# A hybrid decoder trunk in float32: the table load for Exp and Ln is queued behind all Silus of the mixers

## The chip, the cores and the metric

The kernel runs on one core of one Trainium2 chip. The metric is the device time of one execution in microseconds (us); the time before is the median of three runs. Durations come from one profiled execution of the same program. In the profile PE is TensorE's matmuls, PEld its weight loads, DVE is VectorE, ACT is ScalarE, POOL is GpSimd. L384 is line 384 of the kernel.

## The reference

The input is one sequence of 256 tokens of width 1024 in float32. Two layers follow each other; each is

```python
x = x + 0.5 * swiglu(rms_norm(x, ffn1_norm), w_gate, w_up, w_down)      # inner width 2816
P = rms_norm(x, mix_norm) @ w_in                                        # 3608 columns, cut among four mixers
y = concat[gla(P_a), fox(P_b), ssd(P_c), short_conv(P_d)] @ w_out
x = x + y
x = x + 0.5 * swiglu(rms_norm(x, ffn2_norm), w_gate, w_up, w_down)
```

The mixers need two families of functions. Silu is wanted four times in the state-space mixer and the gated linear attention: on the convolved columns of x, B and C (`silu(conv(xbc) + b)`), on the gate z, and on the gate g of the linear attention. Exp and Ln are wanted in all four mixers: softplus (as max(w, 0) + ln(1 + exp(-|w|))), the decays, the softmax of the forgetting attention, and the inverse root of every headwise RMS norm (exp(-0.5 ln(.))).

## The kernel before, in words

Everything lies with features on the partitions and the 256 tokens in the free dimension. Each weight block of 128x1024 float32 is loaded by SyncE's queue, rounded by ScalarE to a high part `wh` (the CAST at L120) and reduced by VectorE to the rest `wl` (L122); a product is then three matmuls of rounded parts: high by high, high by low, low by high (`mm3`, L138; `wide`, L155 and L158, for the feed-forward parts). These two operations for each block run through the whole kernel.

A layer is `ffn`, `mixing`, `ffn`. `mixing` walks through 15 projections in the order PROJ (c_x, c_B, c_C, small, c_z, a_g, b_q, ...). After each projection is traced, `advance()` lets each of five Python generators (`narrow`, `ssd`, `fox`, `gla`, `shortconv`) trace its next piece, up to its next `yield`. So the mixers' small work stands among the projections' matmuls. That is only the order in which the program is traced. The order on each engine is made by a planner that simulates the program (`schedule_with_timeline_sim=True`, L1016) and moves instructions within what the data and extra order edges allow. An extra edge is made by `tc.issue_after(ins)`: what is traced in its block is queued behind `ins` on the engine of `ins`. `tc.keep_in_program_order(ins)` queues `ins` behind the one instruction of its engine that was traced last. Each engine then works its queue in order.

ScalarE looks up a function in the table set that is active. A load of a set is an instruction of its own (ACT_TABLE_LOAD). Three kinds of them stand in the program. The kernel asks for two itself: the set of Silu at the start (L82), and in each layer `natural_log_exp_and_others` by `load_exp_ln` (L379 and L380). The others are put in after the planner, ahead of an instruction whose function the active set does not serve; the profile gives them the line of that instruction (L322, L484 for Silu, L384 for Exp and Ln).

The part of a mixer that matters here, in the order of tracing:

- `ssd` (L473): `conv(i)` (L477) does two blocks of 128 columns each: a scaling on ScalarE (L480), three multiply-adds on VectorE (L482), Silu on ScalarE (L484). `conv(0)`, `conv(1)`, `conv(2)` are traced while the projections c_C, small and c_z stand in line; then follow the Silu of z (L497), that of g (L500), and `load_exp_ln()` (L501), which is thereby pinned behind the Silu of g alone. It then sets `ready["exp"]`.
- `narrow` (L449) waits for `ready["exp"]` and traces the softplus of the narrow columns (L457: Abs at L389, Exp, Ln, then VectorE at L392), the coefficient (L459), the product and scan that give `cs` (L461, L462), `Ra` (L466), and four scalings that give `La` (L468).
- Every Exp and Ln goes through `expln` (L382), which queues it behind the load.
- `ssd` then multiplies `La` with `Ra` on TensorE (L537); `fox` makes its scores, their row maximum `mx` (L631), the exponentials `pr` (L634, shown under L384) and their transposes on TensorE (L643).

Of the kernel before, what the change touches and what calls it, by code (L numbers as in the profile page):

```python
# [11 lines left out]
AF = mybir.ActivationFunctionType  # L12
# [50 lines left out]
def tile_kernel(tc, xT, W, WS, gains, params, consts, out):  # L63
    nc = tc.nc
    with ExitStack() as ctx:
# [8 lines left out]
        V, S, TE = nc.vector, nc.scalar, nc.tensor  # L74
# [299 lines left out]
            return xn  # L374


        loaded = [None]

        def load_exp_ln():  # L379
            loaded[0] = tc.keep_in_program_order(S.preload_act_table_set("natural_log_exp_and_others")).ins  # L380

        def expln(*args, **kw):  # L382
            with tc.issue_after(loaded[0]):
# [11 lines left out]
        def mixing(l, xs):  # L395
# [9 lines left out]
            def P(name, n=1, i=0):  # L405
                o = PCOL[name] + i
                return par[:, l, o:o + n]

            def wait(name):
                while name not in ready:  # L410
                    yield

            def evict(name, dst=None, **kw):
                if dst is None:
                    dst = t2(name, **kw)
                V.tensor_tensor(dst, ready[name], bc2(rbc), op=ALU.mult)
                return dst
# [55 lines left out]
            def ssd():  # L473
# [3 lines left out]
                def conv(i):  # L477
                    for c in (2 * i, 2 * i + 1):
                        a = xbc[:, c, :]
                        S.activation(a, U[:, c, 0:T], AF.Copy, scale=P("cw", 1, c))  # L480
                        for k in range(1, 4):
                            V.scalar_tensor_tensor(a, U[:, c, k:k + T], P("cw", 1, 6 * k + c), a,  # L482
                                                   op0=ALU.mult, op1=ALU.add)
                        S.activation(a, a, AF.Silu, bias=P("cb", 1, c))  # L484

                for i, name in enumerate(("c_x", "c_B")):
                    yield from wait(name)
                    evict(name, U[:, 2 * i:2 * i + 2, 3:])
                conv(0)
                yield from wait("c_C")  # L490
                evict("c_C", U[:, 4:6, 3:])
                conv(1)
                yield
                conv(2)
                yield from wait("c_z")
                sz = evict("c_z")
                S.activation(sz, sz, AF.Silu)  # L497
                yield from wait("a_g")
                sg = sh["sg"] = evict("a_g")
                S.activation(sg, sg, AF.Silu)  # L500
                load_exp_ln()  # L501
                ready["exp"] = True
                yield from wait("cs")
# [266 lines left out]
            def shortconv():  # L770
# [21 lines left out]
                y[3] = hilo(yd)  # L792

            mixers = [narrow(), ssd(), fox(), gla(), shortconv()]

            def advance():
# [224 lines left out]
```

## Time and profile before

| | |
|---|---|
| median of three runs | 1038.33 us (1036.86, 1038.33, 1040.24) |
| the profiled execution | 1035.23 us |
| its span, first to last instruction | 1033.4 us |
| mean granted TensorE clock over the span | 0.995 |
| busy share PE, DVE, ACT | 98%, 74%, 59% |
| first mixing stage, about | 200 to 332 us of the span |
| second mixing stage, about | 712 to 840 us of the span |

A timeline row reads: start, length, engine, line, operation, out<-in, shapes, count, and in brackets the idle time of the engine ahead of it and what ended that. A row with a count above one joins neighbours, so its length is that of the whole.

### The profile page before, as it was taken

Reading aid. Unit: us, or ns where it says so; the run is one execution under the profiler, and the core shown is the slowest. Engines: PE = TensorE matmul, PEld = TensorE weight load, DVE = VectorE, ACT = ScalarE, POOL = GpSimd, SP = SyncE. Lnnn points to the kernel's source line nnn. Section 1 sums busy time; section 2 is a strip of 40 time slices with the busy share of each in tenths; the row PEclk is TensorE's granted clock in tenths of the full one; section 3 lists DMA queues with packets and bytes.
Section 4 is the critical chain, followed back from the end, with each engine's and each line's share of the span. In section 5 each row is a group of like instructions: output and inputs, shape, how many; then the busy total and the mean of one; then the engine's idle time right before and its main releaser. Section 6 shows DMA issues by size and latency. Waiting matters only on the chain.

```text
span 1033.4 us, 16590 instructions
## 1 busy us (share of the span) xinstructions
PE 1014.7 (98%) x6424; PEld 911.8 (88%) x6424; DVE 763.9 (74%) x1192; ACT 612.8 (59%) x928; POOL 1.8 (0%) x6
## 2 busy tenths in 40 slices
PE   7999999999999999999999999999999999999998
PEld 5888888998989888888888888889989998888887
DVE  7987856695877888775688877567868779877652
ACT  6655644469768665554365555344798676555430
POOL 0000000000000000000000000000000000000000
PEclk9999999999999999999999999999999999999999
DMA  8756555372435466554656555564624337665550
GB/s 294 265 196 186 188 197 186 104 258 88 144 102 164 151 222 196 186 186 145 219 187 200 184 185 186 180 204 131 217 93 136 120 122 242 194 188 191 185 180 24
DMA packets 62462, 181.52 MB, mean 176 GB/s; under 512 B 5808, under 2 KB 6960, under 8 KB 62384
## 3 DMA queue, kind: packets, MB, share of 16 engines
q1 hardware_dynamic: 62240, 180.44, 52.9%
q8 instruction: 50, 0.82, 0.3%
q14 instruction: 28, 0.23, 0.1%
q10 hardware_dynamic: 144, 0.02, 0.0%
HBM read 179.40 MB, written 1.05 MB: 175 GB/s over the span
## 4 chain that ended last, share of the span: by engine, by line
PE 91%; ACT 6%; DVE 2%; issue 1%; DMA 0%; ACTq 0%; DVEq 0%
PE acc L155 29%; PE ps L155 18%; PE acc L158 15%; PE ps L138 9%; PE ps L158 9%; PE acc L138 7%; ACT wh L120 2%; ACT L384 1%; DVE wl L122 1%; PE acc L654 1%; DMA x<-xT 0%; PE acc L718 0%; PE acc L537 0%; PE acc L643 0%; PE acc L626 0%
## 5 line engine op out<-in xcount | busy, mean ns | idle before, releaser
L120 ACT CAST wh<-st 128x1024 fp32r<-128x1024 f32 (+1 forms) x339 | 352.2, 1047 | 323.8 <-PE acc L155 135.7
L122 DVE TENSOR_TENSOR wl<-st,wh 128x1024 fp32r<-128x1024 f32 (+1 forms) x339 | 409.8, 1218 | 167.7 <-ACT wh L120 167.0
L155 PE MATMUL acc<-xs,wh 128*128 128x512 f32 x880 | 313.0, 398 | 7.0 <-DVE xs L210 7.0
L158 PE MATMUL acc<-xs,wl 128*128 128x256 f32 x880 | 246.1, 281 | 0.2 <-DVE wl L122 0.2
L155 PEld LDWEIGHTS acc<-xs,wh 128*128 128x128 f32 x880 | 165.6, 188 | 45.3 <-ACT wh L120 6.8
L155 PE MATMUL ps<-xs,wh 128*128 128x512 f32 x528 | 189.2, 397 | 0.0
L158 PEld LDWEIGHTS acc<-xs,wl 128*128 128x128 f32 x880 | 166.6, 189 | 2.2 <-DVE wl L122 1.3
L155 PE MATMUL acc<-h,wh 128*128 128x512 f32 x440 | 158.5, 396 | 0.0
L158 PE MATMUL ps<-xs,wl 128*128 128x256 f32 x528 | 147.5, 280 | 0.7 <-DVE wl L122 0.7
L138 PE MATMUL ps<-xs,wh 128*128 128x256 f32 x672 | 126.2, 288 | 0.0
L158 PE MATMUL acc<-h,wl 128*128 128x256 f32 x440 | 123.3, 280 | 0.0
L155 PEld LDWEIGHTS ps<-xs,wh 128*128 128x128 f32 x528 | 99.1, 188 | 23.1 <-ACT wh L120 0.2
L138 PEld LDWEIGHTS ps<-xs,wh 128*128 128x128 f32 x672 | 105.8, 192 | 0.9 <-issue 0.3
L158 PEld LDWEIGHTS ps<-xs,wl 128*128 128x128 f32 x528 | 99.6, 189 | 1.3 <-DVE wl L122 0.9
L155 PEld LDWEIGHTS acc<-h,wh 128*128 128x128 f32 x440 | 82.6, 188 | 19.5
L155 PE MATMUL ps<-h,wh 128*128 128x512 f32 x264 | 96.8, 396 | 0.0
L138 PE MATMUL ps<-xs,wl 128*128 128x256 f32 x336 | 95.5, 286 | 0.0
L158 PEld LDWEIGHTS acc<-h,wl 128*128 128x128 f32 x440 | 82.9, 189 | 0.0
L158 PE MATMUL ps<-h,wl 128*128 128x256 f32 x264 | 74.0, 280 | 0.0
L138 PEld LDWEIGHTS ps<-xs,wl 128*128 128x128 f32 x336 | 64.2, 192 | 0.3
L155 PEld LDWEIGHTS ps<-h,wh 128*128 128x128 f32 x264 | 49.6, 188 | 11.7
L158 PEld LDWEIGHTS ps<-h,wl 128*128 128x128 f32 x264 | 49.8, 189 | 0.0
(229 smaller groups left out, 1126.8 us busy)
## 6 DMA issues: line engine op xcount, KB each, us to landing
st<-W SPq DMA_DIRECT2D x335, 512.0 KB, 3.6
x<-xT SPq DMA_DIRECT2D x4, 256.0 KB, 4.9
st<-WS SPq DMA_DIRECT2D x2, 512.0 KB, 3.5
out<-x SPq DMA_DIRECT2D x8, 128.0 KB, 1.9
cst<-consts SPq DMA_DIRECT2D x1, 652.0 KB, 8.6
st<-W SPq DMA_DIRECT2D x2, 256.0 KB, 4.4
par<-params SPq DMA_DIRECT2D x1, 308.0 KB, 8.6
cst<-consts SPq DMA_DIRECT2D x1, 128.5 KB, 5.9
```

The costliest lines, as they stand in the source:

```text
L120: S.copy(hi, src)
L122: V.tensor_tensor(lo, src, hi.bitcast(F32), op=ALU.subtract)
L138: TE.matmul(ps, u[sa], v[sb], start=first and i == 0, stop=last and i == 2, skip_group_check=True)
L155: TE.matmul(flat(ps), wh, flat(b), start=first, stop=False, skip_group_check=True)
L158: TE.matmul(ps[:, 0, :], wl, b[:, 0, :], start=False, stop=last, skip_group_check=True)
L384: S.activation(*args, **kw)
L654: TE.matmul(po8[:, 4 * t + h, :], pT[:, t + k, h, :], vb[:, k, 64 * h:64 * h + 64], start=first, stop=k == t, skip_group_check=True)
```

## The change

The Silus of a layer's mixers are collected in a list when they are traced (`conv` six times, z once, g once: eight instructions), and `load_exp_ln` queues the table load behind each of them. It stays pinned behind the last traced instruction too. The list is emptied for the next layer. Nothing is computed differently; every edge is one of issue order on ScalarE.

```diff
-        loaded = [None]
+        loaded, silus = [None], []
+
+        def silu(dst, src, **kw):
+            silus.append(S.activation(dst, src, AF.Silu, **kw).ins)
 
         def load_exp_ln():
-            loaded[0] = tc.keep_in_program_order(S.preload_act_table_set("natural_log_exp_and_others")).ins
+            with ExitStack() as behind:
+                for ins in silus:
+                    behind.enter_context(tc.issue_after(ins))
+                loaded[0] = tc.keep_in_program_order(S.preload_act_table_set("natural_log_exp_and_others")).ins
+            silus.clear()
...
-                        S.activation(a, a, AF.Silu, bias=P("cb", 1, c))
+                        silu(a, a, bias=P("cb", 1, c))
...
-                S.activation(sz, sz, AF.Silu)
+                silu(sz, sz)
...
-                S.activation(sg, sg, AF.Silu)
+                silu(sg, sg)
                 load_exp_ln()
```

## Rows read from the trace of the kernel before

**Rows 1.** The page's busy time by engine (share of the span, instructions).

```profile
PE 1014.7 (98%) x6424; PEld 911.8 (88%) x6424; DVE 763.9 (74%) x1192; ACT 612.8 (59%) x928; POOL 1.8 (0%) x6
```

**Rows 2.** Waits of PE over the span: us in total, times, longest.

```profile
PE acc L155 <- DVE xs L210: 7.0, 2, 6.8
PE acc L537 <- ACT La L468: 4.0, 2, 2.0
PE acc L643 <- ACT pr L384: 2.2, 1, 2.2
PE ps L158 <- DVE wl L122: 0.7, 1, 0.7
```

**Rows 3.** Windows: length, busy per engine, PEclk (granted clock), DMA share, GB/s.

```profile
243.00:251.00 8.00, 5.97 (x36) 5.58 (x35) 5.51 (x9) 7.87 (x14) 0.00 (x0) 0.79 0.19 68
248.00:249.00 1.00, 1.00 (x7) 1.00 (x7) 0.15 (x1) 0.99 (x3) 0.00 (x0) 0.50 0.00 0
284.00:292.00 8.00, 5.77 (x37) 5.01 (x36) 4.33 (x7) 7.97 (x19) 0.00 (x0) 0.79 0.19 66
754.00:763.00 9.00, 6.97 (x42) 6.38 (x41) 5.51 (x9) 8.87 (x15) 0.00 (x0) 0.81 0.21 60
```

**Rows 4.** Timeline of PE at the waits of the first mixing stage.

```profile
245.68 3.88 PE L537 MATMUL acc<-Ra,La 128*128 128x128 f32 x16 [2.03 <-ACT La L468]
...
286.75 0.55 PE L643 MATMUL acc<-cst,pr 128*128 128x128 f32 x2 [2.23 <-ACT pr L384]
```

**Rows 5.** Groups of ACT by line: table loads of the whole span.

```profile
L384 ACT ACT_TABLE_LOAD x32 | 41.1, 1283 | 0.6
...
L484 ACT ACT_TABLE_LOAD x2 | 2.6, 1283 | 0.0
```

**Rows 6.** Timeline of ACT, first mixing stage, from the last Silus to La.

```profile
231.81 0.62 ACT L500 ACTIVATE a_g<-a_g 128x512 f32<-128x512 f32 x1
232.45 1.28 ACT L380 ACT_TABLE_LOAD   x1
233.74 0.42 ACT L384 ACTIVATE e_sp_e<-e_sp_e 128x256 f32<-128x256 f32 x1
...
234.27 1.28 ACT L484 ACT_TABLE_LOAD   x1
235.57 0.51 ACT L484 ACTIVATE xbc<-xbc,par 128x256 f32<-128x256 f32 x1
...
237.03 1.28 ACT L384 ACT_TABLE_LOAD   x1
238.33 0.42 ACT L384 ACTIVATE e_sp_e<-e_sp_e 128x256 f32<-128x256 f32 x1
...
243.21 1.28 ACT L384 ACT_TABLE_LOAD   x1
...
245.04 2.06 ACT L468 ACTIVATE La<-cs,cst 128x256 f32<-128x256 f32 x4
```

**Rows 7.** Timeline of DVE, first mixing stage: last conv step, scan, Ra.

```profile
228.40 0.47 DVE L482 SCALAR_TENSOR_TENSOR xbc<-U,par,xbc 128x256 f32<-128x256 f32 x1
...
240.81 0.69 DVE L462 TENSOR_TENSOR_SCAN cs<-cst,cs 128x256 f32<-128x256 f32 x1
...
244.37 0.41 DVE L466 TENSOR_SCALAR Ra<-cs,cst 128x256 f32<-128x256 f32 x1
```

**Rows 8.** Timeline of ACT, first mixing stage, up to the softmax that PE waits for.

```profile
268.61 1.28 ACT L384 ACT_TABLE_LOAD   x1
...
280.45 0.37 ACT L384 ACTIVATE pr<-acc,mx 128x128 f32<-128x128 f32 x1 [4.38 <-DVE mx L631]
...
282.00 1.28 ACT L384 ACT_TABLE_LOAD   x1
...
284.94 1.28 ACT L384 ACT_TABLE_LOAD   x1
286.23 0.37 ACT L384 ACTIVATE pr<-acc,mx 128x128 f32<-128x128 f32 x1
```

## The prediction, made before the change was run

> **What bounds the kernel now.** I read the page's busy line first: PE is busy for 1014.7 of 1033.4 us, ACT for 612.8 [rows 1]. So a change on ScalarE can pay only where PE stands still or runs slowly because of ScalarE. Next come the waits of PE [rows 2]. The largest, 7.0 us, is at the start of a pass over x (VectorE's `xs`) and has no Exp or Ln ahead of it; I leave it as it is. The next two are this change's ground: twice 2.0 us for `La`, once in each layer, and once 2.2 us for the softmax rows `pr`. Both releasers are ScalarE instructions that stand behind table loads. Together 4.0 + 2.2 = 6.2 us.
>
> A wait of PE costs more than its length here. In the stretches around the three waits the mean granted clock is 0.79, 0.79 and 0.81 [rows 3]. The low part comes when the wait is over and PE is busy: the microsecond from 248 is at 0.50 with PE busy in all of it [rows 3], inside the L537 row, 16 matmuls in 3.88 us behind an idle time of 2.03 us [rows 4]. So at the lower of the two levels (1.2 instead of 2.4 GHz) PE loses 0.21 x 8 = 1.68, 0.21 x 8 = 1.68 and 0.19 x 9 = 1.71 us of work, in all 5.07 us. The mean clock of the whole span agrees: 0.005 x 1033.4 = 5.2 us, so nothing else in the kernel runs slowly. What these three waits cost is 6.2 + 5.1 = 11.3 us.
>
> **What the change removes.** The groups of ACT show 32 table loads ahead of Exp and Ln, 2 ahead of Silu at L484, and the 2 that the kernel asks for at L380, 1283 ns each [rows 5, 6]. The timeline shows how they come about. The load at L380 is at 232.45, and the Exp at 233.74 runs under it without another. Then one Silu of `conv(2)` stands behind them: a load at 234.27 gives it its set back, and the set that held Exp and Ln together is lost. From there each passage from Exp to Ln or back has a load of its own: 16 in each layer. With the load at L380 behind all eight Silus, no Silu follows, and the set stays until the next feed-forward part asks for Silu. So (32 + 2) / 2 = 17 loads leave each layer. One occupies ScalarE for 233.74 - 232.45 = 1.29 us, so 22 us go from each layer and 44 us in all. ACT's busy time should end near 612.8 - 43.6 = 569 us.
>
> Only the loads ahead of PE's waits count. Four removed loads stand between the load at L380 and `La` (234.27, 237.03, 243.21 and one more of the same form between the last two): 5.2 us. The moved Silu itself runs before the load and not after it, so its 0.5 us is spent either way. `La` thus could start at 245.04 - 5.2 = 239.8. Two inputs of the product are VectorE's: the scan that makes `cs` ends at 241.5, and `Ra` at 244.8 [rows 7]. The scan hangs on the Ln at 238.33, which has two removed loads ahead of it: it ends near 238.9. `Ra` stands behind a low part whose CAST has three ahead of it: near 240.9. PE comes to L537 at 245.68 - 2.03 = 243.65. So `La`, `Ra` and `cs` are some 2.5 us early where `La` was 2 us late, and the wait goes; what is late next is nothing that I can name. Layer 2 shows the same order and the same wait of 2.0 us.
>
> For `pr` both sides move. PE will come 2.0 + 1.7 = 3.7 us earlier, since its first wait is gone, so `pr` must come 2.2 + 3.7 = 5.9 us earlier. Between `La` and the `pr` row at 286.23 stand seven removed loads, of which [rows 8] shows the last three: 9.1 us, and 5.2 us before them. Part of that is not passed on, because ScalarE is idle for 4.4 us at 280.45, waiting for the row maximum. But that maximum hangs on the norm of the keys, behind the load at 268.61 and three more before it (5.2 us with it, on top of the four ahead of `La`), and the loads at 282.00 and 284.94 stand between it and the `pr` that PE wants: another 2.6 us. So this wait goes too, unless VectorE, busy with other work, passes on under 3.3 us of what precedes.
>
> **What it adds.** The load now waits for the last Silu of `conv(2)` in ScalarE's order, and every Exp and Ln of the layer, and `La` and `pr` through them, is queued behind it. The last VectorE step of that Silu's input ends at 228.9 [rows 7], 3.6 us before the load at 232.45, and the Silu of g, behind which the load stands already, begins at 231.81. So in the order of before the Silu fits between them and the added wait is zero; at most it is the Silu's own 0.5 us, which its move has paid. No DMA, semaphore or byte is added. SyncE's queue has no step moved past it. The CASTs of weights (L120) share ScalarE and come up to 5 us earlier; their buffers are set free by PE, which bounds them anyway.
>
> The active set must serve all that follows. Exp is seen under the preloaded set [rows 6]; Ln under it is not seen in any row, as each Ln of before has its own load. The sum takes it that Ln is served, by the set's name in the code; the case that it is not is a rival below. The Trainium skill, "ScalarE: Activation LUTs", section "Table sets: the hidden batching unit", says that this set holds both and that Ln followed by Exp takes one load. No row of before shows that; by it all 17 loads go.
>
> **The sum.** Made against the profiled execution, 1035.23 us: 1035.23 - 11.3 = 1023.9. The median shown is 3.1 us above that execution, so the same saving puts the median at 1038.33 - 11.3 = 1027.0. I forecast 1027. The bounds of the saving: it ends at 11.3 + 0.7 (PE's next wait, for `wl`) on the one side; on the other it is what remains if a wait stays.
>
> **The rivals.**
> - *A new wait takes the place of one or two old ones.* The planner writes the order anew once the edges are there, and its order is not that of the chip: it put a Silu whose input was there at 228.9 behind Exps at 233.74 [rows 6, 7]. PE works its queue in order, so one instruction placed early costs a wait. By the three at hand one costs 2.0 to 2.2 us without and 3.7 to 3.9 us with the slow clock behind it; both prices stand, because the wait of 0.7 us [rows 2] has no slow clock behind it (the three stretches use up the mean of the span). With one or two of them: 1027 + 2.0 = 1029 to 1027 + 7.8 = 1034.8. Against it: ScalarE gains 22 us in stages where it was busy for 7.9 of 8 us around the waits [rows 3]. The Trainium skill, "TensorE: Matmul & The Clock Gate", section "What's actually happening", says that the chip watches activity in a rhythm of its own that does not start with the kernel; by that one and the same wait could cost either price from run to run, where the trace has the slow clock behind three of three.
> - *The loads stay.* If the set did not serve Ln, only the load at L484 would go from each layer, and a load would still stand ahead of each passage. Then `La` is 1.3 us earlier, the two waits at L537 fall from 2.0 to 0.7 us, and the gain is 2.6 us, or 2.6 + 3.4 = 6.0 with the clock: 1035.7 to 1032.3. The Exp that runs without a load under the set, and the set's name, speak against it.
> - *The gain is given back in full.* Three new waits of the old kind: 1038, no change.
> - *Slower: the Silu comes late, and everything behind it.* The place is the last Silu of `conv(2)`. If the new order puts its three VectorE steps behind other work (low parts of 1.2 us, evictions of 0.7), the load and with it all Exps start later by as much. The first 2.5 us are covered by the lead of `La`. From there PE waits at L537, in both layers. To be slower than before by 3 us the two layers must lose 14.3 us, 7.2 each, of which 1.7 is clock: a wait of 5.5 us, so the Silu would have to be 8 us later than in the trace. At 10 us it is 2 x (7.5 + 1.7) - 11.3 = 7 us slower, 1045. The steps end 3.6 us before the load now starts, so I give it little.
>
> **How the numbers follow.** Forecast 0.62; a new wait or two 0.21; the loads stay 0.05; given back in full 0.06; slower 0.06. About 0.3% (3.1 us) is what a measurement of this kernel can tell from no change. Faster is the first two and most of the third, 0.62 + 0.21 + 0.04 = 0.87; the same is 0.07, slower 0.06. The range's upper end is 1035, the end of the second case, above which the last cases lie. The lower end is the forecast from the profiled execution, with PE's small wait gone and 1.5 us for the distance between the median and the lowest of the runs shown: 1023.9 - 0.7 - 1.5, about 1021.5.
>
> **What would show it.** The groups of ACT: no ACT_TABLE_LOAD at L384 and L484, two at L380, two at L322; ACT near 569 us. The waits of PE: none for `La` and `pr`. The windows of the mixing stages: a granted clock of 1.0, and 0.999 or more over the span. Wrong would be a new wait of PE above 1 us in a mixing stage, loads that still stand at L384, or PE work that takes longer with no wait in sight, which I have no row for.

## The result and the profile after

The changed kernel takes 1021.26 us (median of four runs, 1020.04 to 1026.31), the kernel before 1039.28 (four runs, 1036.86 to 1042.18). The ratio is 0.9857, 95% interval 0.9823 to 0.9891: faster by 1.4%. The profiled execution takes 1022.20 us against 1035.23, 13.0 us less (ratio 0.9874), where 11.3 had been worked out. The median lies 0.24 us below the lower end of the range; 1038.33 x 0.9857, the ratio on the median that stood ahead of the prediction, is 1023.5. Three executions of two experiments below (one of e1_loads_back, two of e7_loads_late) ran at a mean granted clock of 0.57 to 0.85 and took 1094 to 1681 us, and the ratios leave them out.

The page's busy line answers to [rows 1]: 44 us less on ACT, as worked out (569), 34 instructions fewer, and 6.4 us less on PE with the same 6424 matmuls.

```profile
PE 1008.3 (99%) x6424; PEld 907.7 (89%) x6424; DVE 763.6 (75%) x1192; ACT 569.5 (56%) x894; POOL 1.8 (0%) x6
```

All waits of PE after (us in total, times, longest), to be read beside [rows 2]. The waits for `La` and `pr` are gone, no other has come, and the one at the start of a pass is nearly as it was (6.6 us, 7.0 before).

```profile
PE acc L155 <- DVE xs L210: 6.6, 1, 6.6
PE ps L158 <- DVE wl L122: 0.7, 1, 0.7
PE acc L278 <- DVE dg L274: 0.4, 1, 0.4
PE acc L158 <- DVE wl L122: 0.2, 1, 0.2
```

All table loads of the kernel after, by line (L386 is the load that waits for the Silus). The 32 at L384 and the 2 at L484 of [rows 5] have no successor.

```profile
L386 ACT ACT_TABLE_LOAD x2 | 2.6, 1283 | 0.0
L322 ACT ACT_TABLE_LOAD x2 | 2.6, 1283 | 0.0
L82 ACT ACT_TABLE_LOAD x1 | 1.3, 1283 | 0.7 <-PEq L1019 0.7
```

The timeline of ACT after, the stretch of [rows 6] (the new lines stand 7 lower; a Silu has the line of its helper, L380). The last Silu of `conv(2)` is at 232.24 instead of 235.57, the load follows it, Ln (235.40) runs without one, and `La` starts at 239.75, where the prediction had 239.8.

```profile
231.72 0.61 ACT L380 ACTIVATE a_g<-a_g 128x512 f32<-128x512 f32 x1
232.24 0.49 ACT L380 ACTIVATE xbc<-xbc,par 128x256 f32<-128x256 f32 x1
232.76 1.28 ACT L386 ACT_TABLE_LOAD   x1
234.05 0.42 ACT L391 ACTIVATE e_sp_e<-e_sp_e 128x256 f32<-128x256 f32 x1
...
235.40 0.41 ACT L391 ACTIVATE e_sp_e<-e_sp_e 128x256 f32<-128x256 f32 x1
...
237.41 0.63 ACT L391 ACTIVATE e_gc_e<-e_gc_e 128x512 f32<-128x512 f32 x1
...
239.22 0.63 ACT L391 ACTIVATE e_gc_e<-e_gc_e 128x512 f32<-128x512 f32 x1
239.75 2.07 ACT L475 ACTIVATE La<-cs,cst 128x256 f32<-128x256 f32 x4
...
276.66 0.40 ACT L391 ACTIVATE pr<-acc,mx 128x128 f32<-128x128 f32 x1
```

PE after, at the product of `Ra` and `La` ([rows 4]), and windows of the stretches of [rows 3]. The product follows its predecessor at once and takes 1.95 us for what took 3.88; PE is busy in all of the windows at full clock.

```profile
243.40 1.95 PE L544 MATMUL acc<-Ra,La 128*128 128x128 f32 x16
```

```profile
243.00:251.00 8.00, 8.00 (x71) 8.00 (x70) 5.30 (x10) 7.94 (x14) 0.00 (x0) 1.00 0.28 81
284.00:292.00 8.00, 8.00 (x80) 7.64 (x80) 4.77 (x14) 1.50 (x4) 0.00 (x0) 1.00 0.42 132
```

Where the 13 us went can be read off PE's timeline stage by stage. The table gives, for the kernels of this study, the time from the start of the first transposition in a mixing stage (L513 of before) to the end of the last output product, and its parts: "to La" from the transposition of `bt` (L524) to the product with `La` (L537), "La to ecs" from there to the product with `ecs` (L555), "to scores" on to the scores of `fox` (L626), "to pr" on to the last row of transpositions of `pr` (L643).

| kernel, layer | stage | to La | La to ecs | to scores | to pr |
|---|---|---|---|---|---|
| before, 1 | 101.4 | 4.5 | 8.0 | 21.8 | 14.9 |
| before, 2 | 97.2 | 4.5 | 8.2 | 20.7 | 12.2 |
| after, 1 | 92.8 | 2.3 | 6.1 | 21.4 | 10.9 |
| after, 2 | 92.8 | 2.3 | 6.1 | 20.7 | 12.2 |
| e1_look, 1 | 99.9 | 4.5 | 7.6 | 22.3 | 13.4 |
| e1_look, 2 | 97.1 | 4.5 | 8.2 | 20.7 | 12.3 |
| e6_first_layer, 2 | 97.0 | 4.5 | 7.6 | 21.2 | 12.3 |
| e7_loads_late, 1 | 96.1 | 2.3 | 6.1 | 22.2 | 13.4 |
| d2_two_loads, 2 | 94.2 | 2.3 | 6.9 | 21.2 | 12.2 |
| d3_three_loads, 2 | 95.6 | 3.1 | 7.6 | 21.2 | 12.3 |

The first stage gains 8.6 us, the second 4.4; together 13.0, the whole difference of the two profiled executions. What stands between the two stages (410.1 us) and behind the second (191.5 us) takes the same time before and after. In other executions these parts differ by up to 2 us (189.5 behind the second stage in e1_look, e6, e7 and d3), so the stages are compared below and not only the totals.

### The profile page after: what moved, and what is told of

The parts are those of the page before. It is cut to its first block, busy times and chain, and to the rows that moved or that the text cites. A ratio compares the mean times of both kernels' runs of the same rounds, so it can differ in the third digit from the quotient of the medians.

```text
span 1020.4 us, 16556 instructions
## 1 busy us (share of the span) xinstructions
PE 1008.3 (99%) x6424; PEld 907.7 (89%) x6424; DVE 763.6 (75%) x1192; ACT 569.5 (56%) x894; POOL 1.8 (0%) x6
## 4 chain that ended last, share of the span: by engine, by line
PE 97%; DMA 1%; DVE 1%; ACT 1%; issue 0%; DVEq 0%
PE acc L155 29%; PE ps L155 18%; PE acc L158 15%; PE ps L138 14%; PE ps L158 9%; PE acc L138 7%; DMA cst<-consts 1%; PE acc L633 1%; PE acc L661 1%; PE acc L448 0%; DMA x<-xT 0%; ACT wh L120 0%; PE acc L544 0%; PE acc L725 0%; PE acc L574 0%; PE acc L650 0%
## 5 line engine op out<-in xcount | busy, mean ns | idle before, releaser
L120 ACT CAST wh<-st 128x1024 fp32r<-128x1024 f32 (+1 forms) x339 | 352.8, 1048 | 340.4 <-PE acc L155 135.5
```

The source lines that it names most:

```text
L120: S.copy(hi, src)
```

## The experiments

**Loads or order?** Besides the loads, the change moved the Silu on ScalarE, and on PE three of the products of B and C in each layer (L517 of before) stand 14 matmuls, about 1.8 us, earlier; e1's expectation calls them transposes. VectorE's order is the same. Two kernels separate loads and order: one has the new order with the loads, one the old order without.

**e1_loads_back**, on the changed kernel:

```diff
-                expln(coef, P("alog"), AF.Exp)
+                expln(coef, P("alog"), AF.Silu)
```

> The changed kernel, with one word edited: the coefficient's Exp, second instruction behind the load, is a Silu (so the decays of the state-space mixer are other numbers). The order on every engine stays that of the changed kernel, but the set is lost again and 17 loads in each layer come back. Theory A (the loads that nobody planned for hold up La and pr, PE waits and then runs at the slow clock): as the kernel before, 1035 for the profiled run, ratio 0.99 to 1.00 to it; PE waits near 2.1 us for La in both layers and 2 us for pr in the first; mean clock 0.995; ACT 613 us busy. Theory B (the gain is the new order: the Silu and three transposes stand earlier): 1022, ratio 0.986, no such waits.

Measured: ratio to the kernel before 0.9994 (0.9968 to 1.0021); 34 loads at L391, 43.6 us, are back. The whole gain is gone with every engine's order as in the changed kernel. The waits of PE are read from e1_look, below.

**e5_no_last_silu**, on the kernel before:

```diff
-                        S.activation(a, a, AF.Silu, bias=P("cb", 1, c))
+                        S.activation(a, a, AF.Silu if c < 5 else AF.Identity, bias=P("cb", 1, c))
```

> The kernel before, with the last Silu of conv(2) replaced by Identity with the same bias (that block of C is left without its Silu). The order on every engine is that of the kernel before, and the 17 loads of a layer are gone, as no Silu follows the load. Theory A: as the changed kernel, 1022 to 1023 profiled, ratio 0.986, no PE wait for La or pr, clock 1.0. Theory B: as the kernel before, 1035, ratio 1.00.

Measured: ratio 0.9877 (0.9847 to 0.9906), profiled 1026.20. No wait for `La` or `pr`. Both mixing stages take 92.8 us, as after; its profile lost 4 us ahead of the first stage, in a feed-forward part that the edit doesn't touch. The old order without the loads has the gain of both stages. Theory B falls; the loads are the cause.

**e6_first_layer**, on the changed kernel:

```diff
-        def load_exp_ln():
+        def load_exp_ln(l):
...
-                for ins in silus:
+                for ins in silus if l == 0 else ():
```

> The change in the first layer alone; the second layer's load is pinned as before. Theory A: the first layer gains 8.6 to 8.7 us (a wait for La, a wait for pr, the slow clock behind both), the second nothing, where the whole change has 4.3 there: 1022.2 + 4.3 = 1026.5 profiled, ratio 0.990, one PE wait of 2.0 us for La. A rival that the stages share their gain evenly (half of 13) gives 1028.7.

Measured: ratio 0.9911 (0.9881 to 0.9940), profiled 1026.48. The split is as expected, 97.0 us for the second stage. But the row of the product and the window around it, timeline and windows of this kernel in the second layer, show something that the theory did not hold:

```profile
750.65 2.59 PE L544 MATMUL acc<-Ra,La 128*128 128x128 f32 x16 [2.03 <-ACT La L475]
...
754.17 0.39 PE L535 MATMUL acc<-cst,dte 128*128 128x4 f32 x2 [0.57 <-DVE dte L514]
```

```profile
747.00:756.00 9.00, 6.39 (x48) 5.60 (x47) 5.51 (x9) 8.88 (x15) 0.00 (x0) 1.00 0.18 60
```

The wait is the 2.03 us of before, but the clock stays at 1.00, and the stage still takes 97.0 us where the one with the slow clock took 97.2.

**e7_loads_late**, on the changed kernel:

```diff
-                expln(dte, cs[:, 0:128], AF.Exp, scale=-1.0, bias=cs[:, 127:128])
+                expln(dte, cs[:, 0:128], AF.Silu, scale=-1.0, bias=cs[:, 127:128])
```

> The changed kernel with the Exp of dte made a Silu (other numbers in that decay). It is the first instruction behind La, so no load comes back ahead of La, and 14 in each layer behind it, up to and past pr. Order on every engine as in the changed kernel. Theory A with the lead of pr as in the trace: no wait for La in either layer; pr in the first layer waits again, 2.5 us, and the slow clock costs 1.8 more: 1026.5 profiled, ratio 0.990; nothing in the second layer. If only the loads ahead of La matter: 1022. Theory B: 1022 too, but then e1 is at 1022 as well.

Measured: ratio 0.9885 (0.9851 to 0.9919), profiled 1023.75. No wait for `La`, and the one for `pr` in the first layer, as expected (its waits of PE):

```profile
PE acc L650 <- ACT pr L391: 2.3, 1, 2.3
```

So the loads ahead of `La` and those behind it each cost a wait of their own. The slow clock expected behind this one stayed away: the mean over the span is 1.0, and "to pr" is 13.4 us, where it was 14.9 with the slow clock.

**What does the slow clock cost?** **e1_look** is e1_loads_back in another execution.

> The kernel of e1_loads_back once more, for its trace, as the profiled execution there ran throttled from end to end. As there: PE waits near 2.0 us for La in both layers and about 2.2 us for pr in the first, profiled 1031 to 1036. New question, since e6 had a 2.03 us wait for La at full clock: if the slow clock is what the wait costs beyond its length, the stretch from the first product of Ra and La to the product with ecs takes 8.0 us where the clock falls and 6.3 us where it does not; if PE is held up there by La's later parts and by dte in any case, it takes 7.6 us at full clock, as in e6.

Measured: 1031.35. The waits of PE for `La` and `pr`, and windows behind the three, in the order La, pr, La:

```profile
PE acc L544 <- ACT La L475: 4.0, 2, 2.0
PE acc L650 <- ACT pr L391: 2.3, 1, 2.3
PE acc L535 <- DVE dte L514: 0.6, 1, 0.6
...
PE acc L574 <- DVE xd L551: 0.4, 1, 0.4
```

```profile
244.00:252.00 8.00, 6.03 (x45) 5.45 (x46) 4.45 (x9) 7.89 (x14) 0.00 (x0) 1.00 0.23 68
284.00:292.00 8.00, 5.74 (x48) 5.00 (x48) 4.58 (x8) 7.97 (x20) 0.00 (x0) 1.00 0.22 66
753.00:762.00 9.00, 6.98 (x43) 6.44 (x42) 5.46 (x9) 8.89 (x14) 0.00 (x0) 0.81 0.18 60
```

One wait for `La` in one execution has the slow clock behind it, the other does not. With it "La to ecs" and "to scores" take 8.2 + 20.7 = 28.9 us, and 8.0 + 21.8 = 29.8 in the first layer of before; without it 7.6 + 22.3 = 29.9 in the first layer and 7.6 + 21.2 = 28.8 in the second of e6. Within 0.2 us the slow clock behind `La` costs nothing. Behind `pr` it costs 14.9 - 13.4 = 1.5 us.

**before_again** is the kernel before in another execution.

> The kernel before, unchanged, looked at once more. If the slow clock belongs to a 2 us wait, the three stretches behind the waits for La, pr and La again are at 0.8 once more and the profiled execution takes 1035. If it comes or stays away by itself (it came behind three of three in the kernel before, behind one of three in e1_look), some stretch is at 1.0, and the stages show what it costs net: by e1_look and e6 a wait for La costs 4.2 to 4.5 us with and without it, the wait for pr 2.5 without and 4.0 with it.

Measured: 1035.55, waits of 2.0, 2.2 and 2.0 us and clocks of 0.79, 0.81 and 0.81, each within 0.1 us in every column of the table. So this kernel had the slow clock behind the same three waits in both profiled executions, e1_look behind one of three, e6 and e7 behind none: whether it comes hangs on more than the length of the wait.

**e10_first_part** asks why the slow clock costs nothing behind `La`. On e1_loads_back:

```diff
-                        TE.matmul(ps[:, h, :], La[:, h, 128 * c:128 * c + 128], Ra[:, 128 * c:128 * c + 128],
+                        TE.matmul(ps[:, h, :], La[:, 0, 128 * c:128 * c + 128], Ra[:, 128 * c:128 * c + 128],
```

> The kernel of e1_loads_back, and each product with Ra takes the first part of La in place of its own (the decays of three heads are wrong), so that PE no longer waits for La's parts two to four; the order on every engine is that of e1_loads_back. If those parts are what holds PE up behind its wait at full clock, the stretch from that product to the one with ecs falls from 7.6 to 6.8 us in both layers (with the wait for dte as it was), and the whole by 1.6 us. If PE just meets ScalarE again at its next product, the wait for dte grows from 0.6 to 1.3 us and the stretch stays at 7.6.

Measured, the timeline of PE in the first layer, at full clock, of e1_look and then of e10_first_part:

```profile
245.39 2.59 PE L544 MATMUL acc<-Ra,La 128*128 128x128 f32 x16 [2.02 <-ACT La L475]
...
248.91 0.27 PE L535 MATMUL acc<-cst,dte 128*128 128x4 f32 x1 [0.57 <-DVE dte L514]
```

```profile
245.40 2.05 PE L544 MATMUL acc<-Ra,La 128*128 128x128 f32 x16 [2.02 <-ACT La L475]
...
248.90 0.27 PE L535 MATMUL acc<-cst,dte 128*128 128x4 f32 x1 [1.09 <-DVE dte L514]
```

The product is 0.54 us shorter and the wait for `dte` 0.52 us longer; the product with `dte` starts at the same time, and "La to ecs" stays at 7.5. In the second layer, where the clock was low in both, "La to ecs" and "to scores" take 7.8 + 20.9 = 28.7 us against 28.9. So PE, once it has caught up with a late ScalarE, meets it again at the next product, and the time it saved on the way went into that wait; that a slow clock behind `La` runs down the same waiting time follows from this and from the equal sums above. The whole execution took 1033.17 us, 1.8 more than e1_look, where the first theory had 1.6 less: the mixing stages take 99.8 and 97.0 us, as there or shorter, and the 1.8 us come in the last feed-forward part, which the edit doesn't touch.

**How much lead has La?** **d2_two_loads** and **d3_three_loads**, each on the changed kernel:

```diff
-            expln(e, e, AF.Exp, scale=-1.0)
+            expln(e, e, AF.Silu if tag == "gc_e" else AF.Exp, scale=-1.0)
```

```diff
-            expln(e, e, AF.Ln, bias=1.0)
+            expln(e, e, AF.Silu if tag == "sp_e" else AF.Ln, bias=1.0)
```

> The changed kernel with the Exp of the linear attention's softplus made a Silu (other numbers in its gate). Order on every engine as in the changed kernel. Two loads come back ahead of La (2.6 us), the rest behind it. La's first part ends 3.1 us before PE comes for it in the changed kernel, so no wait for La; pr waits as in e7_loads_late, 2.3 to 2.6 us. 1024 to 1026, ratio 0.988 to 0.990. A theory in which each load costs its 1.3 us on the path would give 1022 + 2 x 2.6 + 2.3 = 1030.

> The changed kernel with the Ln of the narrow softplus made a Silu (other numbers in dt). Order as in the changed kernel. Three loads ahead of La, 3.9 us against a lead of 3.1: a wait for La of 0.8 us in each layer. If beyond the wait PE is held up by La's later parts and dte, 1.3 to 2 us more in each layer, with or without slow clock: 1022.2 + 2 x 2.5 + 2.5 for pr = 1029.7, ratio 0.993. If a short wait costs its length alone: 1022.2 + 1.6 + 2.5 = 1026.3, ratio 0.990.

Measured: d2 0.9934 (0.9911 to 0.9957), d3 0.9943 (0.9922 to 0.9964). Of d3 the waits of PE:

```profile
PE acc L544 <- ACT La L475: 1.2, 2, 0.6
PE acc L535 <- DVE dte L514: 1.1, 2, 0.6
PE acc L574 <- DVE xd L551: 0.7, 2, 0.4
```

d3 went as its first theory had it (profiled 1028.22 against 1029.7): 0.6 us of wait for `La` and 2 us of later meetings in each layer, at a clock of 0.999. d2 was a miss. Its median of 1030.9 falls on the number of the theory that each load costs its length, but not for that reason: there is no wait for `La` ("to La" 2.3). Two things had been left out. With the two loads ahead of `La` and a third ahead of `dte`, `dte` and `xd` come late though `La` does not, 0.6 and 0.4 us, so a stage takes 94.2 instead of 92.8; the load ahead of `dte` alone does not do it, as e7 has that load and no wait for `dte`. And the slow clock came behind `pr` in its profiled execution, for nearly 10 us, longer than behind any other wait in these profiles (windows):

```profile
284.00:294.00 10.00, 10.00 (x49) 8.99 (x48) 6.35 (x10) 5.61 (x14) 0.00 (x0) 0.51 0.53 156
```

PE is busy in all of this window and ScalarE in 5.6 us of it, and here the slow clock does cost time: the first stage takes 101.6 us, where d3 with one load more takes 98.4. The five executions of d2 with a mean clock of 0.998 or more take 1028.4 us in the mean, the five others (0.994 or 0.995, the profiled one among them) 1033.4, so some 5 us go with it.

**e8_known_loads**, on the changed kernel, which gave no answer:

```diff
         def expln(*args, **kw):
-            with tc.issue_after(loaded[0]):
+            with ExitStack() as behind:
+                behind.enter_context(tc.issue_after(loaded[0]))
+                for _ in range(2 if args[2] == AF.Ln else 0):
+                    again = tc.keep_in_program_order(S.preload_act_table_set("natural_log_exp_and_others")).ins
+                    behind.enter_context(tc.issue_after(again))
                 S.activation(*args, **kw)
```

> The changed kernel with two more loads of the same set ahead of each of the eight Lns of a layer, asked for by the kernel and so known to the planner: 16 in each layer as in the kernel before, ACT busy 610 us, and every engine's order planned around them. Theory A1 (what costs is that the plan does not know of the loads): PE's products stand later in its order, waits under 1 us, 1022 to 1027, ratio 0.986 to 0.990. Theory A2 (ScalarE's time in the mixers is what costs, known or not): 1031 to 1035, ratio 0.995 to 1.00.

Measured: ratio 1.0093 (1.0064 to 1.0122), 1048 us, outside both. Of each pair only one load is left, 16 in all, so ScalarE is busy for 590.6 us, 22 less than before, and yet the kernel is 10 us slower than before. The largest wait of PE is a new one:

```profile
PE acc L637 <- DVE KA L625: 10.3, 2, 5.1
```

`KA` is the normed key of the softmax; its last Exp comes at 289.4 us of the span, at 261.8 in the changed kernel. The pins queue each Ln behind what ScalarE was given last in the program, not behind what is ready. The mean clock is lower too, 0.990 in all four executions. So the run doesn't answer whether loads known to the planner could be hidden. It shows that a kernel with half the loads and more edges can be slower; how much of it is the edges themselves and how much the order that the planner made of them is not shown.

## Why the prediction was right, and where its sum was not

**The loads and what they held up.** Right in each step: 17 loads leave each layer, ACT ends at 569.5 us (569), `La` starts at 239.75 (239.8), the waits for `La` and `pr` go, no new one comes. e1 and e5 show that the loads are the cause. That Ln is served by the set, which the Trainium skill states ("ScalarE: Activation LUTs", "Table sets: the hidden batching unit") and no row of before showed, is shown now: Ln at 235.40 runs without a load.

**The length of the waits.** 6.2 us, as in the sum.

**The clock.** This is the term that was mis-sized, and by its cause: 5.1 us were booked for PE at its lower clock behind three waits. The slow stretches are there, but only the one behind `pr` costs time, 1.5 us; behind `La` they cost 0.2 or less each. The sum took lost work of PE for lost time, in a stretch in which PE was not what ended last.

**What was left out.** PE's later meetings with the late ScalarE, which the slow clock had hidden from [rows 2]: a busy PE at half speed shows no wait. Of the 13.0 us, 6.2 are the waits and 1.5 the clock; the rest, 5.3, lies for the most part behind `La`, about 2.5 and 2.3 us in the two layers. Of that the rows of e6 show La's later parts (the product takes 2.59 us instead of 1.95), `dte` (0.6) and `xd` (0.4 in its waits), and leave some 0.7 us unnamed. The two errors, 3.6 too much and 5.3 too little, nearly cancel. That the predicted 11.3 came close to 13.0, with a third of it in the wrong place, is in part luck. The stages' price for `La`, 4.5 and 4.3 us, against 3.7 predicted, shows it without the sum.

**From the profiled execution to the median.** The sum took the same saving for both. By the ratio the median fell by 14.8 us (1038.33 to 1023.5), against 13.0 in the profiles, and the prediction had no row for the difference. The record has the mean clock of 32 further executions of the kernel before: 21 have 0.991 to 0.993 and take 1038.7 us in the mean, five have 0.998 or more and take 1035.5. So most of them were at the low clock for longer than the profiled one (0.995), while the four executions of the changed kernel have 0.999 or 1.000. Some of the median's larger gain is probably this; no trace of such an execution shows where. The lower end of the range adds up to 1021.7 by its own terms, 1023.9 - 0.7 - 1.5, and starts from the profiled execution where the forecast starts from the median.

**The rivals.** No new wait, no load that stays, no late Silu: the last VectorE step of the Silu's input was early, as read. The slower rival's mechanism, an edge that holds back everything behind it, did not come into play; e8, where other edges make `KA` late, fits it without isolating it.

## What to carry to other kernels

A table set that holds all functions of a stage is worth its load only if no function of another set comes after it in the engine's final order, and where a planner writes that order, the load needs an edge behind every instruction of the other set that belongs ahead of the stage. A single stray instruction cost 17 loads of 1.28 us here, and the two mixing stages lost 8.6 and 4.4 us by them. Book a slow clock or a longer instruction as time only where the engine is what ends last; behind a late producer compare the stretch between two meetings, not the engine's busy time.

## What was not expected of the hardware

Behind waits of PE of 2.0 to 2.3 us the granted clock fell to half in some executions and not in others: three of three in both profiled executions of the kernel before, one of three in e1_look and in e10, none in e6, e7 and d3, and behind `pr` in d2 for nearly 10 us. The Trainium skill ("TensorE: Matmul & The Clock Gate", "What's actually happening") has the chip watch activity in a rhythm that does not start with the kernel; the runs do not contradict it: one and the same wait of 2.0 us for `La` has it in e1_look and not in e6. The kernel alone does not decide it either, as the mean clock of the kernel before goes from 0.991 to 1.000 over the 32 executions. What decides in one case stays open.
